# Attention's output kept as features by queries, with its norm's sums taken by matmul and its factors spread through DRAM

## The chip, the cores and the metric

One core of one Trainium2 chip runs the kernel. The time is that of one execution on the device, in microseconds; the number compared is the median of several runs. A profiled execution gives a trace of what each engine did: TensorE (PE, its weight loads PEld), VectorE (DVE), ScalarE (ACT), GpSimd (POOL) and the DMA queue of SyncE (SP).

## What is computed

One transformer layer over 256 context tokens and 2048 latent tokens, width 1024. Of it the change touches the output of differential attention, its norm over the 128 values of a head, and the projection that follows:

```python
def one_block(qblk):
    s = jnp.einsum('bqhmd,bkhmd->bhmqk', qblk, k).astype(jnp.float32) * scale
    p = jax.nn.softmax(s, axis=-1)
    a = p[:, :, 0] - lam * p[:, :, 1]
    return jnp.einsum('bhqk,bkhe->bqhe', a.astype(v.dtype), v)

def merge(attn, four, subln_g, lam_init, w_out):
    b, n = attn.shape[:2]
    a = rms_norm(attn, subln_g) * (1.0 - lam_init)
    return jnp.concatenate([a.reshape(b, n, ATTN_WIDTH), four], axis=-1) @ w_out
```

`four` is the result of a Fourier mixing that is ready before attention. There are 4 heads; latent queries see 512 cached and 2048 own keys, context queries see the 256 context keys. After `merge` comes a gated residual, a second norm and an MLP.

## The kernel before

All work is fp32, split into a high and a low part where three products replace one (`mm3`, L93 to L96). The stages run one after the other: conditioning and input projection, Fourier mixing, attention, output projection, MLP.

*Attention.* For each head the latent queries go in 8 groups of 256 (`Group`), 32 groups in all. Every step of a group is a small function, entered into a list with a due time in units `u` (five to a row, `T`); the list is sorted by due time and written out in that order, so the due time alone sets the order on every engine and queue (L1255 to L1349). Work of neighbouring groups is interleaved. A group covers four rows. In a row TensorE makes five score tiles for a coming group (`fill`, L1080, two records each, 128 x 512 into one of five PSUM banks `S`), VectorE takes a maximum of each (`rowmax`, L1085) and of the five (`comb`, L1088), ScalarE takes the exponentials (`exp`, L1104), which frees the bank. GpSimd combines the two softmax maps into P0 (`combine`, L1111 to L1120). TensorE transposes P0 in pairs of key blocks (`tr`, L1135, into one of two PSUM banks `pt`), ScalarE and VectorE split the transposes (`ah` L1142, `al` L1147), and TensorE multiplies by V (`mul`, L1161 or `mm3`). Rows with two and with three pairs alternate.

The products of a group collect in half of one bank, `po` = `PRO()`, as features by queries. Then, with due times counted from the last row's end, L1335 to L1341: `o1` copies them to SBUF (L1172, ScalarE, 0), `o2` transposes the two halves back to queries by features (L1176, TensorE, 0.4), `o3` copies that to SBUF (L1180, VectorE, 4.25), `o4` squares and sums over a query's features (L1186, ScalarE, 8.5), `o5` makes the factors with a scale-and-add (L1189, VectorE) and a power of -1/2 (L91, GpSimd), `o6` scales the queries and stores them in `att`, 128 tokens by 512 features per tile (L1195, L1196). The last group's steps after `o1` are called by hand within the output projection (`LASTO`).

*Context heads.* `Prompt` does the same for the 256 context queries of a head in the other half of `po`; its products come out as queries by features (L1246), two sets of six per head.

*Output projection.* 18 blocks of 128 tokens. `mix_load` fetches a block of `att` (`am`) and of `four`; `mix` transposes the four 128 x 128 parts of `am` (L1572), copies them with the norm's gain on ScalarE (L1573), and splits the whole for `mm3` (`mh` L1576, `ml` L1577). For the first block this is done at attention's end (`mix0_load`, `mix0_tr`, `mix0_copy`). `w_split` splits the weights (L1544, L1545). Per block: 24 products for one half of the output, the next block's `mix`, the residual (L1595, L1596), the last block's transposes for the MLP (`finish`, L248, from `xn`, L235), 24 products for the other half, residual, norm.

Of the kernel before, what the change touches and what calls it, by code (L numbers as in the profile page):

```python
# [11 lines left out]
F32 = mybir.dt.float32  # L12
# [7 lines left out]
P = 128  # L20
D = 1024
# [16 lines left out]
def f32(ap):  # L38
    return ap.bitcast(F32)


def body(tc, a, out):
    nc = tc.nc
    ctx = ExitStack()
    with ctx:
# [16 lines left out]
        att = [scratch(f"att{i}", [P, 512]) for i in range(NT // P)]  # L62
# [926 lines left out]
        with ExitStack() as c3_:  # L989
# [49 lines left out]
            class Group:  # L1039
# [133 lines left out]

                def o2(self):
                    for j in range(2):
                        nc.tensor.transpose(self.po[:, 256 + j * P:256 + j * P + P], self.oT[:, j * P:j * P + P], ident)  # L1176

                def o3(self):
                    self.o = self.op.tile([P, 256], F32, tag="o", name=f"o{self.nm}")
                    nc.vector.tensor_copy(self.o, self.po[:, 256:512])  # L1180

                def o4(self):
                    osq = self.op.tile([P, P], F32, tag="osq", name=f"osq{self.nm}", bufs=1)
                    self.oss = self.op.tile([P, 4], F32, tag="oss", name=f"oss{self.nm}")
                    for j in range(2):
                        nc.scalar.activation(osq, self.o[:, j * P:j * P + P], AF.Square, accum_out=self.oss[:, j:j + 1])  # L1186

                def o5(self):
                    nc.vector.scalar_tensor_tensor(self.oss[:, 0:2], self.oss[:, 0:2], 1.0 / P, self.s0e, op0=ALU.mult, op1=ALU.add)  # L1189
                    pow_mhalf(self.oss[:, 2:4], self.oss[:, 0:2], 2)  # L1190

                def o6(self):
                    for j in range(2):
                        c = slice(j * P, j * P + P)
                        nc.gpsimd.tensor_scalar(self.o[:, c], self.o[:, c], self.oss[:, 2 + j:3 + j], 0.0, op0=ALU.mult, op1=ALU.add)  # L1195
                        (nc.gpsimd if self.last else nc.sync).dma_start(att[self.hd.tok0 + self.g * 2 + j][:, self.hd.hc], self.o[:, c])  # L1196

            class Prompt(Group):
# [39 lines left out]
                def mul(self, j):  # L1238

                    (ah, al), V = self.A[0], self.hd.V  # L1240
                    n = 0
                    for t in range(2):
                        c = slice((t * 2 + j) * P, (t * 2 + j) * P + P)
                        for l, r in ((ah[:, c], V[:, t, 0, :]), (ah[:, c], V[:, t, 1, :]), (al[:, c], V[:, t, 0, :])):
                            n += 1
                            nc.tensor.matmul(PRO()[:, 256 + j * P:256 + j * P + P], l, r, start=False, stop=(n == 6), skip_group_check=True)  # L1246

                def o3(self):
                    self.o = self.op.tile([P, 256], F32, tag="o", name=f"o{self.nm}")
                    nc.vector.tensor_copy(self.o, PRO()[:, 256:512])  # L1250

# [9 lines left out]
            def load_wout():  # L1261
# [9 lines left out]
                MIX0.extend((f32(ts[0])[:, 2 * D:2 * D + 512], f32(ts[2])[:, 4 * D:5 * D].rearrange("p (k t) -> p k t", t=P)))  # L1271
                nc.sync.dma_start(MIX0[1][:, 4:8, :], four[:, 0:P].rearrange("(k p) t -> p k t", p=P))

            def mix0_load():
                nc.sync.dma_start(MIX0[0], att[0])

            def mix0_tr(gr):
                MIX0.append(gr.bank("pmx0", "pt"))
                for k in range(4):
                    nc.tensor.transpose(MIX0[2][:, k * P:k * P + P], MIX0[0][:, k * P:k * P + P], ident)  # L1280

            def mix0_copy():
# [849 lines left out]
```

## Time and profile before

| | |
|---|---|
| median of 3 runs | 2863.05 us (2862.91 to 2863.21) |
| profiled execution, span from first to last instruction | 2861.4 us |
| TensorE busy | 2831.7 us (99%) |
| VectorE, ScalarE, GpSimd busy | 2018.0, 1548.2, 1073.3 us |
| attention | from about 540 to 1245 us |
| output projection | from about 1245 to 1473 us |

The span is the profiled execution's own time without what lies around it on the device; the runs stand 1.65 us above it. Matmuls are pipelined, so their durations overlap; what one costs is the distance from its start to the start of the next. The granted clock is full throughout.

### The profile page before, as it was taken

The page shows a single profiled execution, that of the slowest core. Times are in us where ns is not written, and L with a number is a line of the kernel's source. Part 1 is how long each engine was busy: PE and PEld are TensorE (multiplying, and loading weights), DVE is VectorE, ACT ScalarE, POOL GpSimd, SP SyncE. Part 2 cuts the span into 40 slices and gives each one's busy share as a digit, 9 for nine tenths or more (in the row PEclk, how much of TensorE's full clock was granted, in tenths as well). Part 3 has the DMA queues.
Part 4 walks back from the last instruction along what each step waited for, and adds up shares of the span by engine and source line. Part 5 has one row for each costly group of instructions (what it writes and reads, how often), then busy time and mean ns, then how long its engine had stood idle before and what let it go on. Part 6 is the DMA issues. An engine that isn't in the chain of part 4 may idle for free.

```text
span 2861.4 us, 43224 instructions
## 1 busy us (share of the span) xinstructions
PE 2831.7 (99%) x15109; PEld 2455.9 (86%) x15109; DVE 2018.0 (71%) x3393; ACT 1548.2 (54%) x3505; POOL 1073.3 (38%) x890
## 2 busy tenths in 40 slices
PE   8999999999999999999999999999999999999999
PEld 5888888688888888888889999999998888888887
DVE  7767886898988989864477777778775354345554
ACT  4333323798989989853356565556555332333221
POOL 1211223798999989942223333333332000000000
PEclk9999999999999999999999999999999999999999
DMA  7776777421211212036767676667747464445663
GB/s 284 219 207 198 230 213 237 172 106 38 73 71 53 106 38 99 23 124 201 242 221 232 223 246 228 221 219 238 234 167 255 147 202 135 138 144 185 206 206 111
DMA packets 392780, 492.94 MB, mean 172 GB/s; under 512 B 26467, under 2 KB 306384, under 8 KB 389490
## 3 DMA queue, kind: packets, MB, share of 16 engines
q1 hardware_dynamic: 387136, 479.73, 50.9%
q0 software_dynamic: 1872, 7.28, 0.8%
q10 hardware_dynamic: 3554, 3.17, 0.4%
q8 instruction: 119, 1.95, 0.3%
q14 instruction: 99, 0.81, 0.1%
HBM read 312.58 MB, written 179.59 MB: 172 GB/s over the span
## 4 chain that ended last, share of the span: by engine, by line
PE 54%; DVE 1%; DMA 0%; ACT 0%; issue 0%; SPq 0%; POOL 0%; DVEq 0%; POOLq 0%
PE ps L94 8%; PE ps L95 8%; PE ps L96 8%; PE pB L1749 2%; PE pB L1747 2%; PE pB L1748 2%; PE pA L1748 2%; PE pC L1748 2%; PE pA L1749 2%; PE pC L1747 2%; PE pA L1747 2%; PE pC L1749 2%; PE po L94 2%; PE po L96 2%; PE po L95 2%; PE pD L1749 1%
## 5 line engine op out<-in xcount | busy, mean ns | idle before, releaser
L1085 DVE TENSOR_REDUCE mxs<-Ss 128x1 f32<-128x512 f32 x636 | 405.4, 686 | 65.5 <-PE Ss L1080 55.1
L1420 DVE TENSOR_TENSOR sl<-sr,sh 128x768 fp32r<-128x768 f32 x168 | 161.8, 964 | 331.5 <-ACT sh L1419 331.1
L1120 POOL TENSOR_TENSOR P0s<-P0s,P1s 128x1024 f32<-128x1024 f32 (+2 forms) x128 | 378.6, 2958 | 10.7
L1419 ACT CAST sh<-sr 128x768 fp32r<-128x768 f32 x168 | 140.6, 838 | 418.3 <-PE ps L95 418.3
L1789 POOL TENSOR_TENSOR gs<-g,g 128x384 f32<-128x384 f32 x48 | 69.7, 1452 | 468.5 <-ACT g L1759 418.9
L1104 ACT ACTIVATE P1s<-Ss,mxs 128x512 f32<-128x512 f32 x318 | 215.4, 694 | 36.3 <-DVE mxs L1088 35.3
L94 PE MATMUL pj<-wh,hh 128*128 128x512 f32 x576 | 228.8, 397 | 2.0 <-DVE hh L555 2.0
L94 PE MATMUL ps<-thT,sh 128*128 128x512 f32 x585 | 227.6, 389 | 0.0
L95 PE MATMUL ps<-tlT,sh 128*128 128x512 f32 x585 | 227.6, 389 | 0.0
L96 PE MATMUL ps<-thT,sl 128*128 128x512 f32 x585 | 227.6, 389 | 0.0
L95 PE MATMUL pj<-wl,hh 128*128 128x512 f32 x576 | 227.1, 394 | 0.5 <-DVE wl L516 0.5
L96 PE MATMUL pj<-wh,hl 128*128 128x512 f32 x576 | 225.6, 392 | 0.0
L1104 ACT ACTIVATE P0s<-Ss,mxs 128x512 f32<-128x512 f32 x318 | 214.3, 691 | 5.6 <-DVE mxs L1088 5.0
L1135 PE MATMUL pts<-ident,P0s 128*128 128x128 f32 x1280 | 191.7, 273 | 4.5 <-DVE als L1147 1.8
L1080 PE MATMUL Ss<-KS0s,Qs 128*128 128x512 f32 x636 | 190.1, 419 | 0.4 <-ACT P1s L1104 0.4
L1080 PE MATMUL Ss<-KS1s,Qs 128*128 128x512 f32 x636 | 188.7, 420 | 1.5 <-ACT P0s L1104 1.4
L1758 ACT ACTIVATE g<-uz 128x384 f32<-128x384 f32 x144 | 75.7, 526 | 200.2 <-DVE uz L1781 174.1
L1135 PEld LDWEIGHTS pts<-ident,P0s 128*128 128x128 f32 x1280 | 151.3, 140 | 35.9 <-issue 4.8
L1119 POOL TENSOR_SCALAR P1s<-P1s,tots 128x1024 f32<-128x1024 f32 (+2 forms) x128 | 171.9, 1343 | 5.8
L1147 DVE TENSOR_TENSOR als<-pts,ahs 128x512 fp32r<-128x512 f32 x256 | 165.9, 681 | 6.9 <-ACT ahs L1142 6.7
L94 PE MATMUL ps<-ophT,sh 128*128 128x512 f32 x423 | 164.7, 389 | 1.1 <-DVE uz L1781 1.1
L96 PE MATMUL ps<-ophT,sl 128*128 128x512 f32 x423 | 164.6, 389 | 0.0
(536 smaller groups left out, 8073.9 us busy)
## 6 DMA issues: line engine op xcount, KB each, us to landing
sr<-sd SPq DMA_DIRECT2D x84, 768.0 KB, 4.5
a<-in_w SPq DMA_DIRECT2D x184, 256.0 KB, 4.2
sd<-gs SPq DMA_DIRECT2D x192, 192.0 KB, 1.9
sd<-g SPq DMA_DIRECT2D x144, 192.0 KB, 2.1
wm<-in_w_mod SPq DMA_DIRECT2D x32, 512.0 KB, 5.2
Qs<-qd SPq DMA_DIRECT2D x32, 512.0 KB, 4.0
b<-in_w SPq DMA_DIRECT2D x64, 256.0 KB, 5.8
b<-tsum SPq DMA_DIRECT2D x64, 256.0 KB, 4.7
```

The costliest lines, as they stand in the source:

```text
L94: nc.tensor.matmul(ps, lh, rh, start=first, stop=False)
L95: nc.tensor.matmul(ps, lh, rl, start=False, stop=False)
L96: nc.tensor.matmul(ps, ll, rh, start=False, stop=last)
L1080: nc.tensor.matmul(S[:, :w], self.Q[:, x, m, j * P:j * P + P], self.hd.KS[m][:, b * 512:b * 512 + w], start=(x == 0), stop=(x == 1))
L1085: nc.vector.tensor_reduce(self.mx[j][:, m, b:b + 1], self.S[j, m, b], axis=AX.X, op=ALU.max)
L1104: nc.scalar.activation(dst, S, AF.Exp, bias=self.mx[j][:, m, 6:7], accum_out=self.sm[j][:, m, b:b + 1])
L1119: nc.gpsimd.tensor_scalar(p, p, tot[:, 3:4], 0.0, op0=ALU.mult, op1=ALU.add)
L1120: nc.gpsimd.tensor_add(d, d, p)
L1135: nc.tensor.transpose(pt[:, c:c + P], self.p0[j][:, (kb + t) * P:(kb + t + 1) * P], ident)
L1747: nc.tensor.matmul(ps, wh[:, c], hh[:, k, :], start=first and k == 0, stop=False, skip_group_check=True)
L1748: nc.tensor.matmul(ps, wh[:, c], hl[:, k, :], start=False, stop=False, skip_group_check=True)
L1749: nc.tensor.matmul(ps, wl[:, c], hh[:, k, :], start=False, stop=k == 3, skip_group_check=True)
```

## The change

The attention output stays as features by queries. Per group: `o1` as before; `oq` squares all 256 columns from SBUF on ScalarE (due 8.5); `o2` multiplies the squares by a column of ones on TensorE, so that the sums of 256 queries come out in two columns of one of the two transpose banks (9.3); `o5` scales and adds from that bank (10.0), `opow` takes the power (10.05); `o6` stores the 256 factors in DRAM (13.0), `o7` loads them back on all 128 partitions (17.5); `o8` multiplies on GpSimd (24.2); `o9` stores features by queries (27.0). The context heads' products are made with 256 columns, six per head instead of twelve, and come out as features by queries too; their copy moves from VectorE to ScalarE, and their later steps to due times a row or more before those of now. In the projection the blocks of `att` are loaded as features by tokens, so the transposes and the copy go, and the gain is folded into the first four of the eight weight blocks.

```diff
-        att = [scratch(f"att{i}", [P, 512]) for i in range(NT // P)]
+        att = [scratch(f"att{i}", [512, 2 * P]) for i in range(NT // 256)]
+        rsd = [scratch(f"rs{h}", [NT // 256, 256]) for h in range(H)]
...
+                def oq(self):
+                    self.osq = self.op.tile([P, 256], F32, tag="P1_1" if self.hd.s else "osq", name=f"osq{self.nm}", bufs=1)
+                    nc.scalar.activation(self.osq, self.oT, AF.Square)
+
                 def o2(self):
+                    self.ps = PRO()[:, 0:2] if self.last else pT.tile([P, 512], F32, tag="pt", name=f"ps{self.nm}")[:, 0:2]
                     for j in range(2):
-                        nc.tensor.transpose(self.po[:, 256 + j * P:256 + j * P + P], self.oT[:, j * P:j * P + P], ident)
-
-                def o3(self):
-                    self.o = self.op.tile([P, 256], F32, tag="o", name=f"o{self.nm}")
-                    nc.vector.tensor_copy(self.o, self.po[:, 256:512])
-
-                def o4(self):
-                    osq = self.op.tile([P, P], F32, tag="osq", name=f"osq{self.nm}", bufs=1)
+                        nc.tensor.matmul(self.ps[:, j:j + 1], self.osq[:, j * P:j * P + P], ones, start=True, stop=True)
+
+                def o5(self):
                     self.oss = self.op.tile([P, 4], F32, tag="oss", name=f"oss{self.nm}")
-                    for j in range(2):
-                        nc.scalar.activation(osq, self.o[:, j * P:j * P + P], AF.Square, accum_out=self.oss[:, j:j + 1])
-
-                def o5(self):
-                    nc.vector.scalar_tensor_tensor(self.oss[:, 0:2], self.oss[:, 0:2], 1.0 / P, self.s0e, op0=ALU.mult, op1=ALU.add)
+                    nc.vector.scalar_tensor_tensor(self.oss[:, 0:2], self.ps, 1.0 / P, self.s0e, op0=ALU.mult, op1=ALU.add)
+
+                def opow(self):
                     pow_mhalf(self.oss[:, 2:4], self.oss[:, 0:2], 2)
...
+                def o6(self):
+                    q, n = self.place()
+                    q.dma_start(rsd[self.hd.h][n].rearrange("(p j) -> p j", j=2), self.oss[:, 2:4])
+
+                def o7(self):
+                    q, n = self.place()
+                    self.rb = self.op.tile([P, 256], F32, tag="P0_1" if self.hd.s else "rb", name=f"rb{self.nm}", bufs=2 if self.hd.s else 1)
+                    q.dma_start(self.rb, rsd[self.hd.h][n:n + 1].partition_broadcast(P).rearrange("p o d -> p (o d)"))
+
+                def o8(self):
+                    q, n = self.place()
+                    v = self.oT.rearrange("p (j t) -> p j t", j=2)
+                    nc.gpsimd.tensor_mul(v, v, self.rb.rearrange("p (t j) -> p j t", j=2))
+
+                def o9(self):
+                    q, n = self.place()
+                    q.dma_start(att[n][self.hd.hc], self.oT)
...
-                def mul(self, j):
+                def mul(self):
 
                     (ah, al), V = self.A[0], self.hd.V
-                    n = 0
                     for t in range(2):
...
+                        c = slice(t * 256, t * 256 + 256)
+                        for n, (l, r) in enumerate(((0, ah), (1, ah), (0, al))):
+                            nc.tensor.matmul(PRO()[:, 256:512], V[:, t, l, :], r[:, c], start=False, stop=(t == 1 and n == 2), skip_group_check=True)
...
-                for t, fn, *args in ((0.25, gp.tr, 0), (0.9, gp.ah), (1.4, gp.al), (15.4, gp.mul, 0), (17.0, gp.mul, 1),
-                                     (20.85, gp.o3), (39.5, gp.o4), (40.2, gp.o5), (40.6, gp.o6)):
-                    add(G[5] + (t - 5 if h == H - 1 and t > 30 else t) * u, fn, *args)
+                for t, fn, *args in ((0.25, gp.tr, 0), (0.9, gp.ah), (1.4, gp.al), (17.0, gp.mul), (20.85, gp.o1), (24.45, gp.oq),
+                                     (25.3, gp.o2), (26.0, gp.o5), (26.05, gp.opow), (29.5, gp.o6), (34.0, gp.o7),
+                                     (40.2, gp.o8), (43.0, gp.o9)):
+                    add(G[5] + t * u, fn, *args)
...
-                    for t, fn in ((0, gr.o1), (0.4, gr.o2), (0.75 if gr.last else 4.25, gr.o3), (8.5, gr.o4), (9.2, gr.o5), (9.6, gr.o6)):
-                        if gr.last and t:
+                    for t, fn in ((0, gr.o1), (8.5, gr.oq), (9.3, gr.o2), (10.0, gr.o5), (10.05, gr.opow), (13.0, gr.o6), (17.5, gr.o7), (24.2, gr.o8), (27.0, gr.o9)):
+                        if gr.last and t > 1:
                             LASTO.append(fn)
...
-            add(base + T + 0.7 * u, mix0_load)
-            add(base + (AVS - 1) * T + 2.5 * u, mix0_tr, gr)
-            add(base + (AVS - 1) * T + 4.45 * u, mix0_copy)
-            
+            add(base + (AVS - 2) * T + 0.7 * u, mix0_load)
...
+                    if k < H:
+                        nc.scalar.activation(wh[k], WOUT[k][:, c], AF.Copy, scale=cols[:, 96:97])
+                        nc.vector.scalar_tensor_tensor(wl[k], WOUT[k][:, c], cols[:, 96:97], f32(wh[k]), op0=ALU.mult, op1=ALU.subtract)
...
             def mix_load(i):
-                am = tx.tile([P, 512], F32, tag="am", name=f"am{i}")
-                nc.sync.dma_start(am, att[i])
-                mT = tx.tile([P, 8, P], F32, tag="mT", name=f"mT{i}")
+                M[i] = mT = tx.tile([P, 8, P], F32, tag="mT", name=f"mT{i}")
+                c = i % 2 * P
+                nc.sync.dma_start(mT[:, 0:4, :], att[i // 2][:, c:c + P].rearrange("(k p) t -> p k t", p=P))
...
             def mix(i):
-                if i == s0:
-                    mT = MIX0[1]
-                else:
-                    am, mT = M[i]
-                    pm = PRO().rearrange("p (k t) -> p k t", t=P)
-                    for k in range(4):
-                        nc.tensor.transpose(pm[:, k, :], am[:, k * P:k * P + P], ident)
-                    nc.scalar.activation(mT[:, 0:4, :], pm, AF.Copy, scale=cols[:, 96:97])
+                mT = MIX0[0] if i == s0 else M[i]
```

## Rows read from the trace of the kernel before

**Rows 1.** Busy time in two stretches: PE, PEld, DVE, ACT, POOL; clock; DMA share, GB/s.

```profile
800.00:900.00 100.00, 99.64 (x637) 83.38 (x637) 88.22 (x175) 89.83 (x254) 90.50 (x74) 1.00 0.12 40
1300.00:1400.00 100.00, 100.00 (x491) 83.81 (x490) 49.49 (x65) 37.11 (x88) 27.73 (x25) 1.00 0.65 205
```

**Rows 2.** TensorE in time order, the row with `o2`: start, duration, engine, operation, [idle].

```profile
816.72 0.71 PE L1080 MATMUL Ss<-KS0s,Qs 128*128 128x512 f32 x2
817.37 0.44 PE L1176 MATMUL po<-ident,oTs 128*128 128x128 f32 x2
817.56 1.22 PE L1080 MATMUL Ss<-KS0s,Qs 128*128 128x512 f32 x4
818.62 0.60 PE L1135 MATMUL pts<-ident,P0s 128*128 128x128 f32 x4
```

**Rows 3.** TensorE in time order, the other three-pair row.

```profile
805.95 1.63 PE L1080 MATMUL Ss<-KS0s,Qs 128*128 128x512 f32 x6
807.42 0.60 PE L1135 MATMUL pts<-ident,P0s 128*128 128x128 f32 x4
```

**Rows 4.** ScalarE in time order, in the row of Rows 2.

```profile
816.94 0.37 ACT L1172 COPY oTs<-po 128x256 f32<-128x256 f32 x1
817.20 0.71 ACT L1104 ACTIVATE P1s<-Ss,mxs 128x512 f32<-128x512 f32 x1
```

**Rows 5.** ScalarE and weight loads in time order, where a score tile waits.

```profile
822.58 0.69 ACT L1104 ACTIVATE P0s<-Ss,mxs 128x512 f32<-128x512 f32 x1
...
823.40 0.30 PEld L1080 LDWEIGHTS Ss<-KS1s,Qs 128*128 128x128 f32 x2 [0.34 <-ACT P0s L1104]
```

**Rows 6.** TensorE in time order, the same row for the first group.

```profile
550.09 1.84 PE L1080 MATMUL Ss<-KS0s,Qs 128*128 128x512 f32 x6
551.77 0.60 PE L1135 MATMUL pts<-ident,P0s 128*128 128x128 f32 x4
```

**Rows 7.** One line's records, ns min/median/max, first and last start.

```profile
L537 PE MATMUL pm<-sums,quad x8: 251/259/259, 29.6 to 30.4; 128*128 128x12 f32 x8
```

**Rows 8.** TensorE in time order, second product set of a context head.

```profile
673.81 0.33 PE L1246 MATMUL po<-Vp,ahp 128*128 128x128 f32 x2
...
674.43 0.68 PE L1080 MATMUL Ss<-KS0s,Qs 128*128 128x512 f32 x2
```

**Rows 9.** DMA issues: queue, count, KB each, median us to landing.

```profile
att<-os SPq DMA_DIRECT2D x62, 64.0 KB, 1.6
```

**Rows 10.** TensorE in time order, the row after a context head's squares.

```profile
700.84 2.06 PE L1080 MATMUL Ss<-KS1s,Qs 128*128 128x512 f32 x6
702.74 0.60 PE L1135 MATMUL pts<-ident,P0s 128*128 128x128 f32 x4
```

**Rows 11.** TensorE in time order, in attention's tail.

```profile
1237.49 1.10 PE L1161 MATMUL po<-ahs,vf4s 128*128 128x256 f32 x4 [0.56 <-DVE os L1180]
```

**Rows 12.** Time order in the output projection: VectorE's norm, then TensorE.

```profile
1313.32 0.75 DVE L235 TENSOR_SCALAR xn<-xo,nrsb 128x1024 f32<-128x1024 f32 x1 [0.66 <-POOL nrsb L91]
...
1314.19 0.60 PE L1572 MATMUL po<-ident,am 128*128 128x128 f32 x4
1314.62 1.04 PE L248 MATMUL ptb<-ident,xn 128*128 128x128 f32 x8
```

**Rows 13.** Time order at the projection's start: VectorE, TensorE.

```profile
1264.73 0.69 DVE L1576 CAST mh<-mT 128x1024 fp32r<-128x1024 f32 x1 [4.22 <-ACT mT L1573]
...
1271.02 1.09 PE L248 MATMUL ptb<-ident,xn 128*128 128x128 f32 x8 [1.56 <-DVE xn L235]
```

**Rows 14.** SyncE's queue in time order: the projection's first load.

```profile
1241.71 0.32 SPq L1560 DMA_DIRECT2D am<-att  x1
```

**Rows 15.** VectorE records of three lines: ns min/median/max, first and last start.

```profile
L1189 DVE SCALAR_TENSOR_TENSOR osss<-osss,s0es x32: 155/440/1367, 582.2 to 1250.7; 128x2 f32<-128x2 f32 x32
...
L1147 DVE TENSOR_TENSOR als<-pts,ahs x256: 676/680/693, 548.9 to 1242.4; 128x512 fp32r<-128x512 f32 x128
...
L1596 DVE TENSOR_TENSOR xo<-xo,gt x36: 691/694/1490, 1258.5 to 1468.5; 128x512 f32<-128x512 f32 x36
```

More of the change, by code (lines that the diff above doesn't have):

```diff
@@ L1188, in o5, with place @@
-                def o5(self):
-                    nc.vector.scalar_tensor_tensor(self.oss[:, 0:2], self.oss[:, 0:2], 1.0 / P, self.s0e, op0=ALU.mult, op1=ALU.add)
+                    nc.vector.scalar_tensor_tensor(self.oss[:, 0:2], self.ps, 1.0 / P, self.s0e, op0=ALU.mult, op1=ALU.add)
+                def opow(self):
                     pow_mhalf(self.oss[:, 2:4], self.oss[:, 0:2], 2)
+                def place(self):
+                    return nc.gpsimd if self.last else nc.sync, self.hd.tok0 // 2 + self.g
@@ L1192, in o6 @@
                 def o6(self):
[L1193 to L1196, printed above, removed]
+                    q, n = self.place()
+                    q.dma_start(rsd[self.hd.h][n].rearrange("(p j) -> p j", j=2), self.oss[:, 2:4])
@@ L1236, in al, with o1 @@
                     self.A[0].append(t)
-                def mul(self, j):
+                def mul(self):
                     (ah, al), V = self.A[0], self.hd.V
-                    n = 0
                     for t in range(2):
[L1243 to L1250, printed above, removed]
+                        c = slice(t * 256, t * 256 + 256)
+                        for n, (l, r) in enumerate(((0, ah), (1, ah), (0, al))):
+                            nc.tensor.matmul(PRO()[:, 256:512], V[:, t, l, :], r[:, c], start=False, stop=(t == 1 and n == 2), skip_group_check=True)
+                def o1(self):
+                    self.oT = f32(at.tile([P, 512], F32R, tag="ahp", name=f"oT{self.nm}", bufs=1))[:, 0:256]
+                    nc.scalar.copy(self.oT, PRO()[:, 256:512])
             ev = []
@@ L1269, in load_wout @@
                     WOUT.append(w)
-                MIX0.extend((f32(ts[0])[:, 2 * D:2 * D + 512], f32(ts[2])[:, 4 * D:5 * D].rearrange("p (k t) -> p k t", t=P)))
-                nc.sync.dma_start(MIX0[1][:, 4:8, :], four[:, 0:P].rearrange("(k p) t -> p k t", p=P))
+                MIX0.append(f32(ts[2])[:, 4 * D:5 * D].rearrange("p (k t) -> p k t", t=P))
+                nc.sync.dma_start(MIX0[0][:, 4:8, :], four[:, 0:P].rearrange("(k p) t -> p k t", p=P))
             def mix0_load():
-                nc.sync.dma_start(MIX0[0], att[0])
-            def mix0_tr(gr):
-                MIX0.append(gr.bank("pmx0", "pt"))
-                for k in range(4):
-                    nc.tensor.transpose(MIX0[2][:, k * P:k * P + P], MIX0[0][:, k * P:k * P + P], ident)
-            def mix0_copy():
-                nc.scalar.activation(MIX0[1][:, 0:4, :].rearrange("p k t -> p (k t)"), MIX0[2], AF.Copy, scale=cols[:, 96:97])
+                nc.sync.dma_start(MIX0[0][:, 0:4, :], att[0][:, 0:P].rearrange("(k p) t -> p k t", p=P))
             for h in range(H):
@@ L1543, in w_split @@
                 for k in range(k0, k1):
-                    nc.scalar.copy(wh[k], WOUT[k][:, c])
-                    nc.vector.tensor_sub(wl[k], WOUT[k][:, c], f32(wh[k]))
+                    if k < H:
+                        nc.scalar.activation(wh[k], WOUT[k][:, c], AF.Copy, scale=cols[:, 96:97])
+                        nc.vector.scalar_tensor_tensor(wl[k], WOUT[k][:, c], cols[:, 96:97], f32(wh[k]), op0=ALU.mult, op1=ALU.subtract)
+                    else:
+                        nc.scalar.copy(wh[k], WOUT[k][:, c])
+                        nc.vector.tensor_sub(wl[k], WOUT[k][:, c], f32(wh[k]))
             def x_load(i):
```

2 lines of the change are left out of this document (removed).

## The prediction

> **What bounds the kernel now.** I read the busy time by stage first. In attention TensorE is busy 99.6% of the stretch at full granted clock (2.4 GHz) with VectorE, ScalarE and GpSimd at 88 to 91%; in the output projection it is busy 100% with the other three at 50% or less [rows 1]. So in the projection a matmul taken away is time taken away. In attention it is not so plain, because four engines run within a tenth of each other. There I read TensorE in order of time: each group of 256 queries takes four rows (two with two pairs of key blocks, two with three), and a row is transposes of P0, ten score records, attention-times-V records. Almost no record is shown as waiting, but the same ten score records don't take the same time in each row, and that difference is what decides.
>
> **The present place of the two transposes is covered.** `o2` (L1176) stands in the row after a group's last products, behind the first score tile. There the first six score records and the two transposes take 1.90 us (816.72 to 818.62), of which the pair itself is 0.19 [rows 2]; in the row two further on the same six take 1.47 (805.95 to 807.42) [rows 3]. So `o2` seems to cost 0.43. But ScalarE runs `o1` (L1172) in just this row, between the second and the third exponential: 0.26 us, and the third exponential ends at 817.20 + 0.71 = 817.91 [rows 4]. The third score tile needs the PSUM bank that this exponential frees. It starts two records before 818.62, at about 818.13, 0.22 us behind it. Where a score tile does wait for an exponential, it goes on 0.13 us behind: the exponential ends at 823.27, the weight load starts at 823.40 after a wait of 0.34 [rows 5]. So without `o2` the third tile could start no sooner than 818.04, and 0.43 us of removed work gives 0.08 us back. The first group confirms it: its row has neither `o1` nor `o2`, and its six score records still take 1.68 (550.09 to 551.77) [rows 6]; with the 0.26 of `o1` that is 1.94, where rows 2 have 1.90.
>
> **The change part by part.**
>
> *Sums of squares by matmul, two rows later.* In place of the two transposes stand two fp32 matmuls with one moving column, in front of the transposes of the row of rows 3. An fp32 matmul is two records on this trace, so four records. No row has one column; with 12 columns eight records start from 29.6 to 30.4, 0.114 each [rows 7], and six 128-column records of another type take 0.62, 0.103 each [rows 8]. Both are near one weight load, so the number of columns won't help: 0.40 for four. Ends: 0.19 (the pair of transposes) and 0.46 (4 x 0.114). In the row of rows 3 no score record waits, so nothing covers it. Twenty-nine of the 32 stream groups have this in the steady part: 29 x (0.40 - 0.08) = **+9.3 us**; ends 29 x (0.19 - 0.08) = +3.2 and 29 x 0.46 = +13.3. The Trainium skill (TensorE: Matmul & The Clock Gate, LDWEIGHTS) says that a weight load takes the number of weight columns over 1.2 in ns, whatever is multiplied by it, 107 ns here: as an estimate four are 0.43 and this term would be +10.2. The row's 0.114 agrees that one column isn't cheaper than twelve.
>
> The sums take a bank of the transposes, of which there are two. The first transposes of the row then need the previous row's second `al`, which today may end after they start, the more so where `o5` stands before it on VectorE; `o5` moves behind it, and the sums in front of the transposes take 0.40 themselves, so I cost this wait at nothing. Where `al` ended 0.5 us later than that, the difference would be lost in each group.
>
> *VectorE, ScalarE, GpSimd.* `o3` goes from VectorE, two squares with their sums become one square of 256 columns, two scalings on GpSimd become one product, and the power -1/2 stays. The square stands at the end of a two-pair row, where two squares stand now and ScalarE then still waits for a maximum. None of these sets TensorE's time in a steady row: 0. If this cover were gone, the square's 0.4 us would show in the next row's score tiles.
>
> *DMA.* Per group two att stores become a factor store, a broadcast load and one att store on SP's queue. Behind them are the next Q loads, three rows ahead of use. An att store lands in 1.6 us [rows 9]; the product on GpSimd comes 14 units of its own work after the power. 0 in the steady part.
>
> *Context heads (4).* Twelve 128-column products per head in two sets of 0.62 [rows 8], 1.30 with re-entry, become six of 256 columns. The six 512-column score records of rows 3 are 0.245 apart, so 0.12 each, 0.73: 4 x -0.57 = -2.3. The squares of the context output now delay the first exponentials of a row in three heads: six score records take 1.90 instead of 1.47 (700.84 to 702.74) [rows 10]; that goes: 3 x -0.43 = -1.3. Their `o1` moves to ScalarE between exponentials, 0.26 as in rows 4: +1.0. Their sums fall in the row which just lost `o2`: +0.2. Together **-2.4**.
>
> *Tail of attention.* No score tiles cover anything there. Gone: the transposes of the first token block (0.43), two waits on `o3` (0.56 is shown for one, 1237.49) [rows 11], two pairs of transposes at 0.45; new: two sums at 0.40. -0.43 - 1.12 - 0.90 + 0.80 = **-1.6**, ends 0 (other engines take over) and -2.5.
>
> *Output projection.* Each token block loses four transposes and the copy after them: 0.43 us (1314.19 to 1314.62) [rows 12], 15 blocks in the steady part, -6.5. What is late next is `xn`: it ends at 1313.32 + 0.75 = 1314.07, 0.12 before the transposes now begin [rows 12], in every second block. I give back 0.3: **-6.2**. At the start three things: the third block's transposes (-0.43); VectorE's `mh` waits 4.2 us for the ScalarE copy of just these transposes and holds up `out_post` and the norm behind it, so that TensorE waits 1.56 us for `xn` [rows 13]: with the block coming by DMA `mh` runs early, -1.6; and the second block's transposes (0.43) with some 0.4 of `o3` on VectorE, which sets that part, -0.8. **-2.8**. The folded scale makes four of the eight splits per half a scalar operation: 0, as the weight products wait for a split only in the first block.
>
> *The queue at the boundary.* The last groups' factors go through DRAM twice, about 4 us more than now, on the queue from which the projection's loads are issued from 1241.71 [rows 14]. If these stand behind the last att store, the second block comes up to 2.9 us late. I take +0.6.
>
> Sum: 9.3 - 2.4 - 1.6 - 6.2 - 2.8 + 0.6 = -3.1 us on a span of 2861.4: 2858.3. The median, 2863.05, is 1.65 above the span, and I keep that: 2860.0.
>
> The Trainium skill (DMA: Bandwidth & Descriptors, Anatomy of one DMA) gives about 2.0 us as the fixed part of any DMA; the 1.6 of rows 9 is lower. By it, as an estimate, the boundary would have 0.8 us more to hide.
>
> **Rivals.**
>
> A. *`o2` isn't covered.* Then its removal gives 0.43, the steady term is 29 x (0.40 - 0.43) = -0.9 and the sum -13.3: 2849.7. Against it are rows 5 and 6; for it, that no wait is shown in rows 2. 0.10.
>
> B. *The one-column records are short*, as the pair of transposes: steady +3.2, sum -9.2: 2853.9. For it: no row has one column. Against: rows 7. 0.17.
>
> C. *Slower: VectorE's scale-and-add (`o5`, L1189) blocks the maxima.* Today it takes 0.16 to 1.37 us, 0.44 in the middle [rows 15], stretched while GpSimd works. It now waits for TensorE and stands in front of a row's five maxima. Ending later than 0.75 us after the sums, it makes the first maximum late; VectorE takes 0.6 a maximum against tiles 0.5 apart, so the delay reaches the fifth, and with it the next row's exponentials and score tiles: up to 0.6 x 29 = 17 us, 2877; with a third of the groups, 2865.8. Against: its large input now lies in PSUM, and `al`, which also reads PSUM and SBUF, took 676 to 693 ns in all 256 cases, while the sum of two SBUF tensors in L1596 went from 691 to 1490 [rows 15]. 0.14.
>
> D. *The projection doesn't give its time*, since `xn` takes the place of the transposes in every second block and the boundary loads come late: -3.1 + 3 + 2.3 = +2.2: 2865.3. 0.14.
>
> **How the numbers follow.** The forecast has 0.45, with its own range 2855 to 2865. About 0.2% (5.7 us) is what a measurement of this kernel can tell from no change: below 2857.3 is faster, above 2868.8 slower. Faster: A, B and 0.07 of the forecast, 0.34. Slower: the larger part of C, 0.10. The same: 0.56. The range is 2852 to 2867: it takes in B, D and the forecast and reaches into C's lower part; A and most of C are left out.
>
> **What would show it.** Right: the four records of the sums about 0.40 apart from the transposes behind them; the six score records of the row that lost `o2` at about 1.82, with a wait for ScalarE, not at 1.47; groups some 0.3 us longer; the projection's blocks 0.43 shorter; no wait at the first norm. Wrong: those six records at 1.47 (A), `o5` over 0.75 us (C), block period unchanged (D), transposes waiting for `al` behind the sums (the bank).

## The result, and the profile after

The changed kernel takes 2867.16 us, the kernel before 2862.96 beside it: a ratio of 1.0015, 95% interval 1.0008 to 1.0021. The forecast was 2860.0, 0.10% below the kernel before, with a range of 2852 to 2867: the time went the other way, by 0.15%, and lies just outside the upper edge. The profiled execution has a span of 2863.3 us; it took 2865.04, 2.1 less than the median. A trace is one execution: those of tail_vector and covered_row2 below took 2.4 and 1.8 us more than their medians, that of tail_queue 2.6 less, so the difference of two traces can stand some us off the difference of the medians.

By stage, cut at records of TensorE: the first transposes of attention, the first transposes of group 30, the first product with the output weights, the first product of the MLP (us, from the two traces):

| stage | before | after | difference | predicted |
|---|---|---|---|---|
| up to attention (unchanged) | 543.84 | 542.04 | -1.8 | 0 |
| groups 0 to 29 | 670.21 | 678.62 | +8.4 | 9.3 - 2.4 = +6.9 |
| tail of attention (groups 30, 31) | 31.17 | 33.79 | +2.6 | -1.6 |
| output projection | 222.34 | 213.71 | -8.6 | -6.2 - 2.8 + 0.6 = -8.4 |
| MLP | 1393.83 | 1395.10 | +1.3 | 0 |

The first line is scatter: in the other kernels below, with the same code up to there, it is 542.8 to 544.8. Seven of the fourteen traces, but not these two, also have a first group of 23.3 to 24.8 us instead of 22.4, with a granted TensorE clock of 0.50 (1.2 GHz) for 3.4 us as attention begins (twice in one of them); that is scatter too. The four other lines add to +3.7, close to the +4.2 of the medians. So the projection came as forecast, and three places have to be explained: 1.5 us in the groups, 4.2 in the tail, 1.3 in the MLP.

*Busy time*, columns as in [rows 1]: TensorE is still the bound in both stretches, with 99.0% and 100%.

```profile
800.00:900.00 100.00, 99.03 (x642) 84.50 (x641) 83.25 (x168) 87.44 (x236) 90.00 (x70) 1.00 0.25 61
1300.00:1400.00 100.00, 100.00 (x475) 83.50 (x474) 44.95 (x66) 33.67 (x83) 24.75 (x24) 1.00 0.68 205
```

*The row that lost the transposes*, in order of time (TensorE, its weight loads, ScalarE), to be read beside [rows 2] and [rows 4]:

```profile
795.99 2.05 PE L1081 MATMUL Ss<-KS0s,Qs 128*128 128x512 f32 x6
797.88 0.60 PE L1136 MATMUL pts<-ident,P0s 128*128 128x128 f32 x4
...
797.31 0.30 PEld L1081 LDWEIGHTS Ss<-KS0s,Qs 128*128 128x128 f32 x2 [0.58 <-ACT P1s L1105]
...
796.46 0.71 ACT L1105 ACTIVATE P1s<-Ss,mxs 128x512 f32<-128x512 f32 x1
```

The exponential ends at 797.17, the weight load of the third tile starts 0.14 later, after an idle 0.58: this wait now stands where the two transposes stood. The six records take 1.89 (795.99 to 797.88), where [rows 2] have 1.90 with the transposes among them; on the mean of 12 groups they take 0.02 less than before.

*The new sums*, ahead of the transposes of the row of [rows 3], and the durations of their parts:

```profile
806.83 0.50 PE L1182 MATMUL pss<-ones,osqs 128*128 128x1 f32 x4
807.19 0.63 PE L1136 MATMUL pts<-ident,P0s 128*128 128x128 f32 x4
807.58 0.70 PE L1081 MATMUL Ss<-KS0s,Qs 128*128 128x512 f32 x2
```

```profile
L1186 DVE SCALAR_TENSOR_TENSOR osss<-pss,s0es x31: 158/159/163, 581.5 to 1249.6; 128x2 f32<-128x2 f32 x31
...
L1182 PEld LDWEIGHTS pss<-ones,osqs x124: 187/192/192, 580.8 to 1249.2; 128*128 128x128 f32 x124
L1182 PE MATMUL pss<-ones,osqs x124: 166/250/250, 580.9 to 1249.3; 128*128 128x1 f32 x124
```

Four records, 0.36 to the transposes; the transposes take 0.39 to the first score tile, where they took 0.35 before (805.60 to the 805.95 of [rows 3]):

```profile
805.60 0.60 PE L1135 MATMUL pts<-ident,P0s 128*128 128x128 f32 x4
```

The steady group (mean distance of the first transposes of 12 groups) goes from 22.01 to 22.39. One such group, from its first transposes to those of the next, before and after:

```profile
789.10 0.60 PE L1135 MATMUL pts<-ident,P0s 128*128 128x128 f32 x4
811.10 0.60 PE L1135 MATMUL pts<-ident,P0s 128*128 128x128 f32 x4
...
790.37 0.60 PE L1136 MATMUL pts<-ident,P0s 128*128 128x128 f32 x4
812.74 0.60 PE L1136 MATMUL pts<-ident,P0s 128*128 128x128 f32 x4
```

*The tail*, in order of time (GpSimd, SyncE's queue, ScalarE, TensorE):

```profile
1236.34 3.49 POOL L1121 TENSOR_TENSOR P0s<-P0s,P1s 128x1536 f32<-128x1536 f32 x1
1239.80 0.73 POOL L1206 TENSOR_TENSOR oTs<-oTs,rbs 128x256 f32<-128x256 f32 x1
...
1231.58 0.32 SPq L1196 DMA_DIRECT2D rs<-ossp  x1
1240.56 0.32 SPq L1210 DMA_DIRECT2D att<-oTs  x1
...
1242.35 0.37 ACT L1173 COPY oTs<-po 128x256 f32<-128x256 f32 x1 [4.17 <-DMA att<-oTs]
...
1239.37 1.47 PE L1136 MATMUL pts<-ident,P0s 128*128 128x128 f32 x12
1242.78 0.39 PE L95 MATMUL po<-ahs,Vs 128*128 128x256 f32 x1 [1.94 <-ACT oTs L1173]
```

It is read from below, from an effect to its cause. TensorE waits 1.94 us to write into `po`, because the copy `o1` of group 30 hasn't read it; the copy waits 4.17 us for an `oT` buffer, from which group 28 is stored only at 1240.56; the store waited for the product `o8` of group 28, and this, which shows no wait of its own, stood behind the last group's combination on GpSimd. SyncE's queue stood still from 1231.9 to 1240.56 behind the same store. In the stretch behind TensorE's wait the granted clock (third column from the right) was 0.62 on the mean, with 0.50 (1.2 GHz) for 3.4 us:

```profile
1240.00:1244.00 4.00, 2.06 (x17) 1.82 (x16) 0.26 (x1) 1.65 (x4) 1.19 (x2) 0.96 0.21 66
1244.00:1248.00 4.00, 4.00 (x21) 3.83 (x21) 2.37 (x4) 1.68 (x4) 0.74 (x1) 0.62 0.12 35
```

The clock is not part of it in each execution. In am_pad and proj_pairs below, whose tail has the same code, TensorE waits about as long there, the clock stays at 1.00, and the tail takes 32.69 and 32.39 us. So of the +2.6 some 1.1 to 1.4 are the clock of this execution, and +1.2 to +1.5 are there without it.

*The projection*: two neighbouring finishes (the transposes for the MLP) are 11.77 apart, 12.25 before, all 14 steady distances alike. Before, where the next finish is the 1314.62 of [rows 12], and after:

```profile
1302.38 1.04 PE L248 MATMUL ptb<-ident,xn 128*128 128x128 f32 x8
...
1308.65 1.03 PE L249 MATMUL ptb<-ident,xn 128*128 128x128 f32 x8
1320.42 1.03 PE L249 MATMUL ptb<-ident,xn 128*128 128x128 f32 x8
```

*The start of the MLP* (ScalarE, TensorE): a wait of the second split `mhh` for VectorE, and two of TensorE, none of which is in the trace before. At the two, TensorE falls behind the trace before by 0.43 and 0.44 us, together with what lies around them 0.98; the other 0.29 of the MLP's 1.27 us lie behind its last product, from whose start to the end 5.05 us pass, and 4.76 before.

```profile
1463.44 1.48 ACT L1480 CAST mhh<-hr 128x1536 fp32r<-128x1536 f32 x1 [1.52 <-DVE mhl L1484]
...
1473.09 0.45 PE L1746 MATMUL pA<-mhh,oplW 128*128 128x384 f32 x1 [0.15 <-DVE oplW L1452]
1475.83 0.44 PE L1745 MATMUL pB<-mhl,ophW 128*128 128x384 f32 x1 [0.55 <-DVE mhl L1484]
```

### The profile page after: what moved, and what is told of

The parts are those of the page before. It is cut to its first block, busy times and chain, and to the rows that moved or that the text cites. A ratio compares the mean times of both kernels' runs of the same rounds, so it can differ in the third digit from the quotient of the medians.

```text
span 2863.3 us, 43138 instructions
## 1 busy us (share of the span) xinstructions
PE 2830.0 (99%) x15093; PEld 2462.1 (86%) x15093; DVE 1982.4 (69%) x3357; ACT 1525.3 (53%) x3383; POOL 1068.7 (37%) x855
## 4 chain that ended last, share of the span: by engine, by line
PE 54%; DVE 1%; DMA 0%; issue 0%; ACT 0%; SPq 0%; POOL 0%; DVEq 0%; POOLq 0%
PE ps L95 8%; PE ps L97 8%; PE ps L96 8%; PE pB L1746 2%; PE pB L1745 2%; PE pB L1744 2%; PE pA L1744 2%; PE pC L1746 2%; PE pA L1745 2%; PE pC L1744 2%; PE pC L1745 2%; PE pA L1746 2%; PE po L97 2%; PE po L95 2%; PE po L96 2%; PE pD L1746 1%
## 5 line engine op out<-in xcount | busy, mean ns | idle before, releaser
L1143 ACT CAST ahs<-pts 128x512 fp32r<-128x512 f32 x256 | 146.7, 607 | 40.9 <-PE pts L1136 40.9
```

## The experiments

All start from the changed kernel. Times are medians, with the ratio to the kernel before and its interval; the changed kernel has 1.0015. The kernel before, measured beside each, took 2862.89 to 2863.66, so differences of under 1 us between two of the times below mean nothing. Edits are cut where `...` stands.

**pair_back**: was the old place covered?

```diff
+def o2old(self):
+    for j in range(2):
+        nc.tensor.transpose(self.po[:, 256 + j * P:256 + j * P + P], self.oT[:, j * P:j * P + P], ident)
-for t, fn in ((0, gr.o1), (8.5, gr.oq), ...
+for t, fn in ((0, gr.o1), (0.4, gr.o2old), (8.5, gr.oq), ...
```

> The changed kernel with the two transposes of the output put back in their old place in the row behind a group's last products, their result unread; everything else stays as changed. Theory: they stand where TensorE has to wait for an exponential anyway, so 29 x 0.02 = 0.6 us, 2867.8. Rival (A of the prediction): they are not covered and cost 0.43 us each time, 29 x 0.43 = 12.5 us, 2879.7.

2869.32 (1.0023, 1.0014 to 1.0032): 2.2 more than the change, not 12.5. The steady group stays at 22.38; 1.7 of the excess are in the tail (33.79 to 35.52), where the pair, too, waits for the late copy. In the row, TensorE in order of time:

```profile
796.85 0.71 PE L1081 MATMUL Ss<-KS0s,Qs 128*128 128x512 f32 x2
797.54 0.44 PE L1177 MATMUL po<-ident,oTs 128*128 128x128 f32 x2
797.73 1.22 PE L1081 MATMUL Ss<-KS0s,Qs 128*128 128x512 f32 x4
798.79 0.60 PE L1136 MATMUL pts<-ident,P0s 128*128 128x128 f32 x4
```

The pair takes its 0.19, and the row is 5.61 long on the mean of 12 groups, 0.02 more than without the pair: rival A is out.

**no_sums**: what do the sums cost?

```diff
-self.ps = PRO()[:, 0:2] if self.last else pT.tile(...)[:, 0:2]
-for j in range(2):
-    nc.tensor.matmul(self.ps[:, j:j + 1], self.osq[:, j * P:j * P + P], ones, start=True, stop=True)
+self.ps = self.osq[:, 0:2]
```

> The changed kernel without the sums of squares on TensorE: the factors are made from two columns of the squares, so the norm is left out of the result. Theory: the four records cost their spacing and the slower start behind them, 0.40 us in each of 36 places, nothing covers them, and nothing waits for their bank: 36 x 0.39 = 14 us less than the change, 2853. Rival: part of the group's 0.38 us is the bank of the transposes that the sums hold; then the row's other records move too and more than 16 us go. Second rival: the row has some cover of its own; then under 8 us go, 2859 or more.

2861.22 (0.9993, 0.9984 to 1.0002): 5.9 less, not 14. The kernel leaves the norm out. The mechanism was right and the sum wrong: the steady group falls from 22.39 to 22.06 and the stage of the groups by 9.7 us, its slow first group included, but the projection becomes 5.8 longer (213.71 to 219.55). Attention ends earlier, TensorE then waits 4.8 us for the split of the projection's first blocks, and behind the wait the granted clock is 0.50 for 3.4 us. This was the first sign that something other than TensorE sets the boundary.

The edit changes one thing more: `o5` reads SBUF, and not PSUM, in the same place. VectorE's records of it:

```profile
L1184 DVE SCALAR_TENSOR_TENSOR osss<-osqs,s0es x32: 149/1028/2034, 584.3 to 1251.6; 128x2 f32<-128x2 f32 x32
```

It took 1028 ns in the middle, where the changed kernel has 159, and in six of 27 groups the row's first maximum starts 1.39 to 1.96 us after `o5` does, in the others 1.00 to 1.07. So the 0.33 us of the group is, if anything, less than the sums cost.

**covered_row** and **covered_row2**: the sums in the place that hides work.

```diff
-self.ps = PRO()[:, 0:2] if self.last else pT.tile(...)[:, 0:2]
+self.ps = PRO()[:, 0:2] if self.last else PRO()[:, 256:258] if self.late else pT.tile(...)[:, 0:2]
+self.late = not hd.s and not (hd.h == H - 1 and g > 4)   # covered_row: 29 of the 32 groups
+self.late = not hd.s and not (hd.h == H - 1 and g > 3)   # covered_row2: 28 of them
-for t, fn in ((0, gr.o1), (8.5, gr.oq), (9.3, gr.o2), ...
+for t, fn in zip((0, 8.5, 20.4, 21.1, 22.1, 25.5, 28.5, 34.2, 36.6) if gr.late else ...   # covered_row
+for t, fn in zip((0, 8.5, 20.6, 21.3, 22.1, 25.5, 28.5, 34.2, 36.6) if gr.late else ...   # covered_row2
-add(base - 14 * T + 0.7 if h else 0.9 * T, hd.load_v)
+add(base - 13 * T + 0.7 if h else 0.9 * T, hd.load_v)    # covered_row2 alone
```

> The changed kernel with the sums of squares of 29 of the 32 groups one row short of a group and a half later: behind the first score tile of the row where the two transposes used to stand, and into the unused half of the products' bank; scale, power, stores and product follow later by as much. The last three groups stay as they are. Theory: that row hides up to 0.41 us of TensorE, so the sums cost 0.02 there and not 0.38: 29 x -0.36 = -10.4 us, 2856.8, which would be 6 us faster than the kernel before. Rival: the cover is not to be had for these four records (their squares, their bank or the scale that reads them come late, or the row in which they stood was hidden after all): no gain, 2867.

2878.09 (1.0051, 1.0038 to 1.0063), a miss with two causes. The sums go into the bank that `o1` reads, and wait until it has: they start 1.0 into the row, 0.05 behind the copy's end, and the row is 0.2 longer than with its bare wait. And a longer chain to the store holds an `oT` buffer longer: in three groups (26.51, 24.17 and 26.02 long) the store came behind the next head's V load on the queue, and in group 28 in the tail (TensorE waits 6.6 us there). The waits view of TensorE in the first of these groups (us in total, times, longest):

```profile
PE po L1183 <- ACT oTs L1174: 2.7, 1, 2.7
```

> The changed kernel with the sums of 28 of the 32 groups in the row of the old transposes as in the run before, but behind the second score tile, so that they needn't wait for the copy o1 that reads the same bank; the next head's V is loaded one row later, behind the store that it held up; the last four groups stay as they are. Theory: the sums then reach 0.10 us past the exponential for which the third tile waits, a steady group takes 22.1 us and not 22.39, and the waits of 2 to 4 us in three groups go: 28 x -0.28 = -7.8 us against the change, 2859.4. Rival: the third tile's slow start behind the sums and the later chain of factors keep the group at 22.2 or more: 2862 or more.

2859.42 (0.9984, 0.9975 to 0.9993), the 2859.4 that was expected. That it agrees so closely is in part luck: in the traces groups 0 to 29 take 8.0 us less than in the change, its slow first group included, and the tail 1.0 less, but the projection 4.3 more, with a wait of 2.1 for the second block's split and a granted clock of 0.50 for 3.4 us behind it. TensorE in order of time, the same row:

```profile
794.87 1.17 PE L1082 MATMUL Ss<-KS0s,Qs 128*128 128x512 f32 x4
795.88 0.50 PE L1183 MATMUL po<-ones,osqs 128*128 128x1 f32 x4
796.24 0.73 PE L1082 MATMUL Ss<-KS0s,Qs 128*128 128x512 f32 x2
796.80 0.60 PE L1137 MATMUL pts<-ident,P0s 128*128 128x128 f32 x4
```

The six score records and the four of the sums take 1.93 together (794.87 to 796.80), 0.04 more than without any; the steady group is 22.02. The same four records cost 0.38 in one row and next to nothing in another (22.02 against 22.01 in the kernel before).

**third_oT** and **tail_vector**: is the tail's wait what the trace says?

```diff
-self.oT = self.op.tile([P, 256], F32, tag="oT", ..., bufs=1 if self.last else 2)
+if self.drain:                                                       # third_oT: group 30
+    self.oT = f32(at.tile([P, 2, 2, 256], F32R, tag="Q", ..., bufs=3))[:, 0, 0, :]
+else: ...
-nc.gpsimd.tensor_mul(v, v, self.rb...)                               # tail_vector: group 28
+(nc.vector if not self.hd.s and self.hd.h == H - 1 and self.g == 4 else nc.gpsimd).tensor_mul(v, v, self.rb...)
```

> The changed kernel with one thing different: the copy o1 of the last group but one writes into a free Q buffer, and not into the oT buffer whose store to DRAM is late. Theory: TensorE's wait of 1.94 us before the products of the second row of the last group's stage in the trace of the change, and the stretch at a granted clock of 0.62 right behind it (some 1.6 us), both come from the copy's wait of 4.17 us for that store. Then about 3.5 us go: 2863.6, that is 0.7 over the kernel before. Rival: the next late thing (the square, a PSUM bank, the products of vf4) takes the wait's place; then less than 1.5 us go, 2865.7 or more.

2883.49 (1.0075, 1.0062 to 1.0087). In attention it did what was expected: the last product of attention comes 29.84 us after the first transposes of group 30, not 33.67. But the projection's `ml` (VectorE, in order of time) now waits for the store from the Q buffer, as if it lay in the same place of SBUF; the projection takes 232.31 us:

```profile
1256.93 0.69 DVE L1576 CAST mh<-wout 128x1024 fp32r<-128x1024 f32 x1 [3.70 <-DMA wout<-att]
1273.61 1.23 DVE L1577 TENSOR_TENSOR ml<-wout,mh 128x1024 fp32r<-128x1024 f32 x1 [15.99 <-DMA att<-oTs]
```

> The changed kernel with one product moved: the scaling o8 of the fourth group from the end (28 of 0 to 31) runs on VectorE, where it needn't queue behind GpSimd's last combination; so its store, and with it the oT buffer, comes free some 7 us earlier. Theory: the copy o1 of group 30 doesn't wait, TensorE's wait of 1.94 us and the slow clock behind it go, and so does the lateness of what stands behind that store on SyncE's queue: 3.8 us less than the change, 2863.4. Rival: the projection then waits for its own loads, which come behind the factors on SyncE's queue (the run without sums showed 4.8 us of waits for the split of the first blocks there), and takes most of it back: 2865.5 or more.

2865.38 (1.0006, 0.9997 to 1.0015): 1.8 less, between the two. The tail falls from 33.79 to 30.02, the 3.8 expected, clock and all; the projection grows from 213.71 to 218.22. Its second block's loads are issued behind the store of group 29 and the factors of group 30, and VectorE, then TensorE, wait for them; behind TensorE's wait the granted clock falls again:

```profile
1251.18 0.32 SPq L1210 DMA_DIRECT2D att<-oTs  x1
1252.37 0.32 SPq L1196 DMA_DIRECT2D rs<-osss  x1
1252.78 0.38 SPq L1566 DMA_DIRECT2D mT<-att  x1
...
1260.54 0.69 DVE L1573 CAST mh<-mT 128x1024 fp32r<-128x1024 f32 x1 [2.52 <-DMA mT<-four]
...
1261.38 0.47 PE L95 MATMUL po<-woh,mh 128*128 128x512 f32 x1 [1.80 <-DVE mh L1573]
...
1263.00:1267.00 4.00, 4.00 (x12) 3.10 (x11) 4.00 (x7) 0.00 (x0) 1.87 (x3) 0.57 1.04 390
```

**tail_queue**: these DMAs on another queue, on top of tail_vector.

```diff
-return nc.gpsimd if self.last else nc.sync, ...
+return nc.gpsimd if not self.hd.s and self.hd.h == H - 1 and self.g > 4 else nc.sync, ...   # groups 29 to 31
```

> The kernel of the run tail_vector with the DMAs of the factors and outputs of groups 29 and 30 on GpSimd's queue, as the last group's are, so that SyncE comes to the projection's loads without them. In tail_vector attention ended 3.8 us earlier than in the change, and the projection was 4.5 us longer. Theory: the loads of the second block stood behind these DMAs; they come some 6 us earlier, the waits of 1.8 and 0.8 us for its splits go, and the gain of the tail is kept: 2863. Rival: they are late for another reason (buffers that attention's tiles hold, the DMA engines themselves): 2865.4, as tail_vector.

2869.47 (1.0021, 1.0013 to 1.0030): 4.1 more than tail_vector, a miss. The wait for the second block's split went (0.2 is left), but GpSimd now stands still 12.5 us at DMAs that wait for each other, and the power of the projection's first norm stands behind them. That is the new wait below; but the projections of the two traces differ by 0.3 only (218.22 and 218.55), so the traces don't account for most of the 4.1.

```profile
1279.41 1.97 PE L249 MATMUL ptb<-ident,xn 128*128 128x128 f32 x8 [4.13 <-DVE xn L236]
```

**proj_pairs**: are the projection's transposes worth their time?

```diff
 def mix(i):
+    if i != s0:
+        pm = PRO().rearrange("p (k t) -> p k t", t=P)
+        for k in range(4):
+            nc.tensor.transpose(pm[:, k, :], mT[:, k, :], ident)
```

> The changed kernel with four transposes put back in front of each of the projection's blocks but the first (of the loaded block, their result unread, without the copy). Theory: TensorE sets the projection, so each costs what it cost before, 0.43 us in 15 blocks of the steady part and two more at the start, 7.3 us, of which the MLP's first products give back the 0.8 us for which they wait for VectorE in the changed kernel: 2873.7. Rival (D of the prediction): the norm or the loads are what is late in every second block, and the transposes are hidden there: less than 3.5 us, 2870.5 or less.

2876.67 (1.0045, 1.0033 to 1.0058): 9.5 more, and not 6.5; 2.0 of it are a wait of the first such transposes for the second block's load. The finishes are 12.25 apart again, as before the change, so a block's transposes are worth 0.47, uncovered: D is out for the steady part. The MLP did not give its 1.3 back (1395.6).

**am_pad** and **both_pad**: does the place of buffers cost the MLP its 1.3 us?

```diff
 def mix_load(i):
+    tx.tile([P, 512], F32, tag="am", name=f"am{i}")
```

> The changed kernel with an unused tile of the old block's size kept in the projection's pool, so that the tiles behind it lie in SBUF where they lay before the change. In the changed kernel ScalarE's second split for the MLP (mhh) waits 1.52 us for VectorE's first (mhl), which it did not before; in program order the second one gained a wait on VectorE, and it loses it with this tile. Theory: the 1.25 us that the MLP takes longer (1395.1 from its first product to the end, 1393.8 before) come from this overlap of buffers and go: 2865.9. Rival: they come from the shorter blocks, which leave VectorE and ScalarE less time for the MLP's splits; then the MLP stays at 1395.1 and the time at 2867.

2873.01 (1.0037, 1.0024 to 1.0049): 5.8 more. The wait of `mhh` for VectorE is gone, and the MLP's first 48 records stand as before the change; then it loses 0.97 at another place, so it is no shorter. There VectorE's `mhl` waits 0.89 us for ScalarE's `mhh`, and TensorE 0.90 for `mhl`: the wait has changed its engine. And the second block's loads are issued behind two more DMAs of group 30, 8.6 us after the projection's first product and not 1.7 ahead of it, so that TensorE waits 6.12 us and then has a granted clock of 0.50 for 6.9 us. The wait in the MLP, then SyncE's queue and TensorE in the projection:

```profile
1488.43 0.45 PE L1746 MATMUL pC<-mhl,ophW 128*128 128x384 f32 x1 [0.90 <-DVE mhl L1484]
...
1264.40 0.43 SPq L1567 DMA_DIRECT2D mT<-att  x1
...
1269.05 0.77 PE L95 MATMUL po<-woh,mh 128*128 128x512 f32 x1 [6.12 <-DVE mh L1574]
```

**both**: tail_vector and covered_row2 in one kernel; both_pad and both_queue add the edits of am_pad, then of tail_queue.

> The two edits of the runs tail_vector and covered_row2 in one kernel. Theory: they touch different stages and add up, -3.8 and -7.8: 2855.6, which is 7.3 us (0.26%) below the kernel before. Rival: attention ends earlier, and the projection's loads, behind the last factors on SyncE's queue, are what is late instead: 2859 or more.

2856.31 (0.9974, 0.9964 to 0.9985): the fastest, 0.26% below the kernel before and 0.7 us above the expected time. Groups 0 to 29 take 668.75 us, the tail 30.57, the projection 215.09. Here TensorE's wait for the second block's split is 0.4 us, and the clock stays at 1.00.

> The kernel of the run both with the unused tile of the run am_pad. Theory: 1.25 us less, 2855.1. Rival: as in am_pad, no difference, 2856.3.

2861.67 (0.9995, 0.9986 to 1.0004). A miss as a whole, by 6.6, but the MLP falls from 1395.09 to 1394.12, and all its 7064 matmul records, counted from its first product, stand within 0.02 us of those before the change; the projection grows by 7.9, as in am_pad.

> The kernel of the run both_pad with the DMAs of groups 29 and 30 on GpSimd's queue, as in tail_queue. Theory: the projection's first waits (0.4 and 0.9 us for the splits of the first two blocks in the run both) shrink by about 1 us: 2854.1, 0.31% below the kernel before. Rival: no difference from both_pad, 2855.1.

2858.90 (0.9985, 0.9977 to 0.9994): better than both_pad, worse than both; the first norm's transposes wait 4.7 us, as in tail_queue. The MLP takes 1394.01, its records again where they were before the change.

## Why the prediction was wrong, step by step

*The old place was covered: right, and more than said.* 0.08 us per group was to come back, 0.02 did: the row lasts 5.59 for 5.61. The third tile starts 0.09 earlier, but behind a wait its second record follows 0.34 later, and not 0.27 (means of 12 groups). The fall of the wait was priced, the slow start behind it was not.

*The sums: right in size.* 0.36 and 0.04 behind them, 0.40 forecast; B is out. The starts of the four lie 0.03, 0.11 and 0.11 us apart, and the transposes follow 0.11 behind the last: but for the first step that is the distance of the records with 12 columns in [rows 7]. The transposes didn't wait for the bank: the second `al` ended 0.17 to 0.23 us before they started. The Trainium skill (TensorE: Matmul & The Clock Gate, LDWEIGHTS) gave 0.43 for the four weight loads, as an estimate: a little high, and nearer than the 0.19 of the pair. With the step above a group costs 0.38 and not 0.32, 29 x 0.06 = 1.8 us more; the context heads gave 0.3 more than the 2.4 forecast, by what is left of the stage's +8.4. covered_row2 shows that the price is that of the place: the prediction saw that the old row hides 0.4 us, and did not see that the new steps could have stood there.

*`o5` (C): out, for the reason given.* It read PSUM and took 158 to 163 ns in 31 cases, where [rows 15] have up to 1367, and ended 0.41 us after the transposes' start on the mean, long before the row's first maximum at 1.14. In no_sums it reads SBUF in the same place and took up to 2034 ns: so it is where the operand lies that counts, and not the place in the row.

*The tail: the step that failed.* It counted TensorE's work and the waits that went, -1.6, with ends 0 and -2.5; +2.6 came, and +1.2 to +1.5 in executions whose clock stayed at 1.00, outside both. What it left out is a lifetime: before, `oT` was last read by the transposes right behind the copy; now it is held until the store `o9` has landed, with the same two buffers. "0 in the steady part" was right, since 8 rows of 5.5 us lie between two uses. But in the tail the rows have no score tiles and last some 3 us, while GpSimd's combinations keep their length: a due time in units is an order, not a time. The product `o8` that was costed at nothing there stood behind 3.49 us of GpSimd's work, on the path of a buffer, a copy, a bank and TensorE. Without that wait the tail takes 30.02 us (tail_vector), -1.2 against the kernel before: the step's own sum was right within 0.5. That the wait comes from this buffer is shown twice, by another buffer for the copy (third_oT) and by an earlier product (tail_vector).

*The projection: right.* 14 steady blocks gave 0.474 each, 6.6 us, and the start 2.0, where 6.2 and 2.2 net were forecast. The 0.3 given back for `xn` was not taken: all blocks are alike. TensorE's wait for the first norm, which was to go, fell from 1.56 to 0.66.

*The boundary (part of D): small in the change, larger where attention ends earlier.* +0.6 was forecast, and the changed kernel shows 0.4 us of waits for splits. There the second block's load is issued 1.7 us ahead of the projection's first product. In no_sums, covered_row2 and tail_vector it is issued 0.1 to 0.3 behind it, and the projection is 4.3 to 5.8 us longer: 1.8 to 4.8 are waits for `mh`, and 3.4 us at a granted clock of 0.50 behind them have their part in the rest. In both it is issued 0.6 ahead, and the projection is only 1.4 longer. So a gain at attention's end was lost again in part, by how the loads stood against it, and the two terms can't simply be added. The prediction's 2.0 us from the Trainium skill (DMA: Bandwidth & Descriptors, Anatomy of one DMA) is given there for DMAs that GpSimd issues; the stores of [rows 9] are issued by SyncE, and no number here rests on it.

*The MLP: not forecast; it stood in no term.* Of its 1.3 us 1.0 go when the projection's pool keeps its old size (both_pad and both_queue against both): the two waits at its start are gone. In am_pad they go too, but another of 0.90 us comes. That the missing tile moved other buffers onto each other fits this, but no run looked at addresses. The other 0.3 us, behind the last product, are not explained.

## What to carry to other kernels

When a step is moved later, list not only who waits for it but which buffer lives longer, and check that lifetime where the rows are shortest, not where they are regular. A matmul has a price only in its row: first find the rows in which TensorE waits for another engine, and put new work there. A gain at the end of a stage can come back as a wait at the start of the next, when the next stage's loads stand on the same queue. And a change of a pool's size can add or remove waits elsewhere: compare the waits of the two builds, stage by stage.

## What the runs showed of the hardware

- A gap can cost more than its length, and not each time. In the changed kernel 2.21 us lie between the starts of two matmuls in the tail, and 0.8 us after TensorE went on the granted clock fell to 0.50 (1.2 GHz), for 3.4 us; in pair_back, with 3.08, it fell too. At the same place am_pad has 2.20, proj_pairs 2.09, covered_row2 2.15 and no_sums 2.63, and their clock stayed at 1.00. In the kernel before and in both no gap of the tail is over 0.86, and the clock stays at 1.00. For am_pad:

```profile
1245.00:1249.00 4.00, 3.74 (x29) 3.64 (x30) 2.25 (x4) 3.07 (x7) 0.74 (x1) 1.00 0.18 46
```

- An fp32 matmul with one moving column is two records, each with a weight load of 187 to 192 ns, and a record starts 0.11 us after the one before (the second of the four 0.03 after the first); with 12 columns [rows 7] it is 0.11 too. So one column costs what twelve do.
- VectorE's scale-and-add of 128x2 took 149 to 1367 ns with both inputs in SBUF in the kernel before and 149 to 2034 in no_sums. With one of them in PSUM, in the same place as in no_sums, it took 158 to 163. Between 800 and 900 us GpSimd was busy 90 to 92% in all three kernels.
